# State space of both layers: products moved from GpSimd to VectorE, responses a step behind their matrices, state copies on ScalarE, first layer's output due inside the first branch

## The chip, the core and the metric

The kernel runs on one core of a Trainium2 chip. Its metric is the device time of one execution in microseconds. The engines are called by the profile's names: PE is TensorE (matmuls; PEld its weight loads), DVE is VectorE, ACT is ScalarE, POOL is GpSimd, SP is SyncE, which here issues nearly all DMAs. An engine runs its instructions in the order in which they were written for it; semaphores join the engines.

## The reference

One inference step of a two-layer model on 128 context tokens and 512 latent tokens, all in fp32, 1024 channels. Per layer: an adaLN modulation, one wide projection, three mixers beside each other (retention, a bidirectional state space model, attention), three branch projections joined by sigmoid gates, an output projection with a LayerNorm, and a gated FFN with a convolution over three tokens and another LayerNorm.

```
z = (x * (1 + sc1) + sh1) @ w_in           # rq rk rv rg | su | nq nk nv | gates
r_out = retention(rq, rk, rv, rg, ...)
s_out = s5(su, ...)
n_out = attention(nq, nk, nv, ...)
m = (ga*(r_out@w_branch[0]) + gb*(s_out@w_branch[1]) + gc*(n_out@w_branch[2])) @ w_o
x = layer_norm(ALPHA*x + g1*m)
f = conv_ffn(x * (1 + sc2) + sh2)
x = layer_norm(ALPHA*x + g2*f)
```

The change is about `s5`: 32 groups of 16 channels, 64 complex states per group and direction. Per group and direction the state follows h(t) = a_bar h(t-1) + b_bar u(t) and the output is Re(C h(t)) + D u(t); then a GELU and a gate `y * sigmoid(y @ w_glu)` (GLU).

## The kernel before

**Main work.** fp32 weights come from HBM as 128x1024 tiles (`raw`), are split into a high part (ACT, L176) and a low part (DVE, L177), and PE multiplies three combinations of parts (L148). A unit of this work is 48 matmuls of 128x320 into one of two PSUM buffers `pa`, then an evacuation on ACT or DVE. `layer` writes down the list of units of a layer: projections for retention and the state space, gates of branch 0, branch 0, GLU, gates and branch 1, attention's projections, branch 2, output projection, FFN.

**Side work.** Retention, attention and the state space are generators. They are carried forward beside the units: each unit has a cost (1 for a usual one), and a generator with rate r makes r steps per unit cost. `RATE_S` is the rate of layer 0's state space, `RATE_P` that of layer 1's preparation (`ssm_prep(1)`), which runs during layer 0's FFN. An action with `need=[ssm]` runs the generator to its end first. A list scheduler then fixes the order of instructions on each engine when the kernel is built; it simulates durations and keeps dependences.

**The state space.** The 640 tokens are cut into 80 chunks of 8. `ssm_powers` computes powers of a_bar. `ssm_entry` (8 batches of 4 groups) makes the matrices that bring a chunk's inputs into the state: six operations of 128x512 (`cmul`, L899 to L904, tiles `eo` and `etm`), then two DMAs to DRAM (`ed`, L1076). In layer 0 these run on DVE except batch 3 (`ENTRY_POOL`), in layer 1 on POOL. `ssm_exit` prepares `bb` by six operations on POOL, then for each batch makes the matrices from states to outputs by six operations of 128x640 on POOL (L1105 to L1110, `go` and `gtm`), stores them (`gd`), and right behind them has PE compute the responses within a chunk from these (16 matmuls, L1119), which DVE collects into `tb` (L1125 to L1129) and SP stores. `ssm_states` multiplies each batch by `ed` on PE (L1161) and copies the results into the state tile H: real parts on DVE (L1167 to L1170), imaginary parts on ACT (L1166). The scan then takes 64 steps of four operations on DVE (L1184 to L1187). `ssm_outputs`: in four groups of eight, H is copied into `hs` (DVE for the real part, ACT for the imaginary one, L1214 to L1218), `gm` is loaded, PE multiplies (L1228, L1230), DVE evacuates into `ym` (L1231), and SP stores eight `yd` (L1235). `ssm_out` loads `yt`, takes the GELU on ACT and splits it (`gyhi`, `gylo`); GLU's matmuls (L1263) read that. In layer 0, `first_ssm` runs the powers, then entry and states beside exit, then the outputs. `ssm_out` is written down behind gate 5 of branch 0.

**Other places of POOL.** Retention's rotation multiplies by the cosine on POOL (L606) and scales queries by decays there (`qd`, L625). In the merge, branch 0's result is written to a tile `mg` by DVE (L1308), branch 1's is added to it on POOL (L1310), branch 2's on DVE (L1312).

In layer 0's FFN the adaLN of layer 1 also runs: weights `in_w_adaT` are loaded as `raw` tiles by SP and multiplied by a row on DVE (L308). The FFN's own evacuation is the convolution (`cv`, L1381) on DVE.

## Time and profile before

| | |
|---|---|
| three runs | 2592.34, 2592.64, 2585.28 us (median 2592.34) |
| profiled execution | 2584.16 us, its span 2582.3, so 1.9 outside the span |
| mean granted clock | 0.974 |
| busy in the span | PE 2416.7 (94%), DVE 1809.3 (70%), ACT 954.7 (37%), POOL 482.5 (19%) |
| instructions | PE 17788, DVE 4043, ACT 1649, POOL 336 |

The stages by time: 0 to 65 us the start; 65 to 402 layer 0's projections, retention and state space; 402 to 968 branches, attention, output projection; 968 to 1240 layer 0's FFN up to its end part; then layer 1, whose states and outputs run beside its projections. A clock of 1.0 in the profile is 2.4 GHz.

### The profile page before, as it was taken

The numbers are of one execution on the slowest core, as the hardware profiler recorded it, in microseconds if no ns is written. First come the engines' busy times: TensorE is split into PE (matmuls) and PEld (weight loads), VectorE is DVE, ScalarE is ACT, GpSimd is POOL, SyncE is SP. The second block draws the span as 40 slices with busy tenths as digits, with TensorE's granted clock in tenths as the row PEclk, the third lists the DMA queues.
The fourth block names the chain that finished last, engine by engine and source line by source line (L and its number), as shares of the span: only waits on it lengthen the run. The fifth ranks groups of instructions, "written<-read, shape, count | busy, mean of one in ns | idle before, by whom it ended". The sixth has DMA issues, their size and how long they took to land. (4 is left out here: it accounts for less than half of the span.)

```text
span 2582.3 us, 45009 instructions
## 1 busy us (share of the span) xinstructions
PE 2416.7 (94%) x17788; PEld 2342.7 (91%) x17788; DVE 1809.3 (70%) x4043; ACT 954.7 (37%) x1649; POOL 482.5 (19%) x336
## 2 busy tenths in 40 slices
PE   7879999899999997989999999989989989999997
PEld 4769999899899997979999999989988989999997
DVE  5997965785367896798665578478545788555657
ACT  3245333136543432313234543421656243232232
POOL 1555101221200007492000210102213200000001
PEclk9889999999999999999999999999999999999999
DMA  8653535552223337345335323555222343222222
GB/s 286 174 173 112 171 95 162 182 162 80 77 91 123 113 108 220 123 131 151 119 99 186 99 92 103 159 176 168 93 87 79 111 127 115 86 62 86 84 76 79
DMA packets 174083, 324.04 MB, mean 125 GB/s; under 512 B 35120, under 2 KB 84528, under 8 KB 173872
## 3 DMA queue, kind: packets, MB, share of 16 engines
q1 hardware_dynamic: 173440, 321.03, 39.5%
q8 instruction: 140, 2.29, 0.4%
q14 instruction: 71, 0.58, 0.1%
q10 hardware_dynamic: 432, 0.13, 0.0%
HBM read 287.09 MB, written 38.21 MB: 126 GB/s over the span
## 5 line engine op out<-in xcount | busy, mean ns | idle before, releaser
L148 PE MATMUL pa<-hth,hi 128*128 128x320 f32 (+2 forms) x2896 | 689.7, 316 | 49.3 <-DVE cv L1381 21.9
L148 PE MATMUL pa<-htl,hi 128*128 128x320 f32 (+2 forms) x2896 | 686.4, 315 | 1.2 <-DVE htl L461 0.8
L148 PE MATMUL pa<-hth,lo 128*128 128x320 f32 (+2 forms) x2896 | 686.0, 314 | 1.5 <-DVE lo L177 1.5
L176 ACT ACTIVATE hi<-raw 128x1024 fp32r<-128x1024 f32 (+1 forms) x316 | 322.2, 1022 | 840.9 <-PE pa L148 336.8
L177 DVE TENSOR_TENSOR lo<-raw,hi 128x1024 fp32r<-128x1024 f32 (+1 forms) x316 | 406.1, 1287 | 289.5 <-ACT hi L176 282.2
L148 PEld LDWEIGHTS pa<-hth,hi 128*128 128x128 f32 x2896 | 496.6, 192 | 59.1 <-issue 26.3
L148 PEld LDWEIGHTS pa<-htl,hi 128*128 128x128 f32 x2896 | 496.3, 191 | 9.1 <-issue 3.0
L148 PEld LDWEIGHTS pa<-hth,lo 128*128 128x128 f32 x2896 | 497.6, 192 | 7.4 <-issue 5.4
L308 DVE SCALAR_TENSOR_TENSOR junk<-raw,crow 128x512 bf16<-128x512 f32 x320 | 249.8, 781 | 53.1 <-DMA raw<-in_w_adaT 48.5
L1338 PE MATMUL b<-lo,hdh 128*128 128x256 f32 x784 | 218.8, 281 | 1.2 <-DVE lo L177 1.1
L1337 PE MATMUL b<-hi,hdh 128*128 128x256 f32 x784 | 216.7, 282 | 3.0 <-DVE rm L1341 1.9
L1339 PE MATMUL b<-hi,hdl 128*128 128x256 f32 x784 | 217.7, 281 | 0.0
L1381 DVE SCALAR_TENSOR_TENSOR cv<-pa,conv,cv 128x641 f32<-128x641 f32 (+3 forms) x180 | 153.1, 852 | 3.6 <-ACT cv L1377 1.5
L1337 PEld LDWEIGHTS b<-hi,hdh 128*128 128x128 f32 x784 | 146.1, 188 | 5.3 <-DVE rm L1341 1.8
L1338 PEld LDWEIGHTS b<-lo,hdh 128*128 128x128 f32 x784 | 147.7, 188 | 1.9 <-DVE lo L177 1.7
L1339 PEld LDWEIGHTS b<-hi,hdl 128*128 128x128 f32 x784 | 147.1, 188 | 0.2 <-issue 0.2
L1341 DVE TENSOR_TENSOR rm<-b,g 128x256 f32<-128x256 f32 x168 | 69.0, 418 | 71.9 <-PE b L1339 69.8
L431 POOL TENSOR_TENSOR x<-x,ln_b 128x512 f32<-128x512 f32 x4 | 6.5, 1660 | 521.2 <-ACT x L430 521.2
L516 PE MATMUL pa<-lo,hth 128*128 128x256 f32 x320 | 91.8, 288 | 2.7 <-DVE lo L177 2.7
L515 PE MATMUL pa<-hi,hth 128*128 128x256 f32 x320 | 93.2, 294 | 1.0 <-ACT rw L1488 1.0
L517 PE MATMUL pa<-hi,htl 128*128 128x256 f32 x320 | 91.2, 288 | 0.0
L176 ACT ACTIVATE hdh<-cv 128x641 fp32r<-128x641 f32 x44 | 32.6, 742 | 143.0 <-DVE cv L1389 132.4
(404 smaller groups left out, 4403.9 us busy)
## 6 DMA issues: line engine op xcount, KB each, us to landing
raw<-in_w_in_a SPq DMA_DIRECT2D x96, 512.0 KB
raw<-in_w_up SPq DMA_DIRECT2D x88, 512.0 KB
raw<-in_w_adaT SPq DMA_DIRECT2D x80, 512.0 KB
raw<-in_w_down SPq DMA_DIRECT2D x36, 512.0 KB
raw<-in_w_branch SPq DMA_DIRECT2D x24, 512.0 KB
raw<-in_w_o SPq DMA_DIRECT2D x24, 512.0 KB
wada<-in_w_ada SPq DMA_DIRECT2D x32, 256.0 KB
raw<-in_w_in_b SPq DMA_DIRECT2D x16, 512.0 KB
```

Of the source, the lines that this page charges most:

```text
L148: s.nc.tensor.matmul(ps[h][:, :n], w[a][:, k], x[b][:, k, c0:c0 + n], start=(k == 0 and part == 0), stop=(k == nk - 1 and part == 2))
L176: s.nc.scalar.activation(hi, src, AF.Copy)
L177: return (eng or s.nc.vector).tensor_tensor(lo, src, hi.bitcast(FT), op=OP.subtract)
L308: nc.vector.scalar_tensor_tensor(junk, w[:, n], 1.0, s.crow[j], op0=OP.mult, op1=OP.mult, accum_out=acc[:, n, j:j + 1])
L515: mm(ps, h[0], x[0], start=(k == 0), stop=False)
L516: mm(ps, h[0], x[1], start=False, stop=False)
L517: mm(ps, h[1], x[0], start=False, stop=(k == 7))
L1337: mm(ps, a[0], x[0], start=(k == 0), stop=False)
L1338: mm(ps, a[0], x[1], start=False, stop=False)
L1339: mm(ps, a[1], x[0], start=False, stop=(k == nk - 1))
L1341: nc.vector.tensor_tensor(m, ps, g[0 if t == 0 else 1][:, 256 * (q % 2):256 * (q % 2) + 256], op=OP.mult)
L1381: nc.vector.scalar_tensor_tensor(x[:, o0:o1], z[:, z0:z0 + o1 - o0], cw(tap), x[:, o0:o1], op0=OP.mult, op1=OP.add)
```

## The change

- Moved from POOL to DVE: the matrices of the exit (`go`, `gtm`, 48 operations per layer), the `bb` preparation (6 per layer), all entry products that were on POOL (6 in layer 0, 48 in layer 1), the product with the cosine (8 per layer) and `qd` (8 per layer), and branch 1's addition (8 per layer).
- `ssm_exit`: matrices of batch b and responses of batch b - 1 make one step; nine steps instead of eight, and `go` of two batches are alive at a time.
- All copies into H and `hs` go to ACT, in both layers.
- Layer 0's `ssm_out` is written down behind the second unit of branch 0, not behind gate 5 (layer 1's stays).
- Branch 0's result stays in its gate tile; the tile for the sum (`ms`) is allocated at branch 1.
- `RATE_S` 1.5 to 1.4 and `RATE_P` 0.6 to 0.5.

```diff
--- before.py
+++ after.py
@@ -605,3 +605,3 @@
             V.tensor_tensor(t1, t1, s.sin, op=OP.mult)
-            G.tensor_tensor(x[:, LP:T], x[:, LP:T], s.cos, op=OP.mult)
+            V.tensor_tensor(x[:, LP:T], x[:, LP:T], s.cos, op=OP.mult)
             V.tensor_tensor(x[:, LP:T], x[:, LP:T], t1, op=OP.add)
@@ -624,3 +624,3 @@
         for d in range(2):
-            G.tensor_tensor(qd[d], q[:, LP:T].rearrange("p (t n) -> p t n", t=4),
+            V.tensor_tensor(qd[d], q[:, LP:T].rearrange("p (t n) -> p t n", t=4),
                             m[:, 2 + d:3 + d].to_broadcast([P, 4, 128]), op=OP.mult)
@@ -1055,3 +1055,2 @@
         nc, V, G, A = s.nc, s.nc.vector, s.nc.gpsimd, s.A
-        on = lambda b: G if l or b in ENTRY_POOL else V
         pd, ed = s.ssm[l]["pd"], s.ssm[l]["ed"]
@@ -1073,3 +1072,3 @@
             tm = s.unit([P, 4, 2, 64], base="etm")
-            s.cmul(on(b), o, pm, [x[:, :, None, :].to_broadcast([P, 4, 2, 64]) for x in be], tm)
+            s.cmul(V, o, pm, [x[:, :, None, :].to_broadcast([P, 4, 2, 64]) for x in be], tm)
             for i in range(2):
@@ -1094,8 +1093,8 @@
             G.memset(bb[i][:, GR], 0.0)
-        s.cmul(G, [x[:, :GR] for x in bb], bs, [f[:, i, :, None].to_broadcast([P, GR, 16]) for i in range(2)], tm)
+        s.cmul(V, [x[:, :GR] for x in bb], bs, [f[:, i, :, None].to_broadcast([P, GR, 16]) for i in range(2)], tm)
         s.free(bs, tm)
         yield
-        for b in range(8):
-            g0 = 4 * b
+        def matrices(b):
 
+            g0 = 4 * b
             o = [s.unit([P, 4, 10, 16], base="go") for _ in range(2)]
@@ -1104,8 +1103,8 @@
             cv = [x[:, g0:g0 + 4, None, :].to_broadcast([P, 4, 10, 16]) for x in ct]
-            G.tensor_tensor(o[0], cv[0], pv[0], op=OP.mult)
-            G.tensor_tensor(tm, cv[1], pv[1], op=OP.mult)
-            G.tensor_tensor(o[0], o[0], tm, op=OP.add)
-            G.tensor_tensor(o[1], cv[0], pv[1], op=OP.mult)
-            G.tensor_tensor(tm, cv[1], pv[0], op=OP.mult)
-            G.tensor_tensor(o[1], o[1], tm, op=OP.subtract)
+            V.tensor_tensor(o[0], cv[0], pv[0], op=OP.mult)
+            V.tensor_tensor(tm, cv[1], pv[1], op=OP.mult)
+            V.tensor_tensor(o[0], o[0], tm, op=OP.add)
+            V.tensor_tensor(o[1], cv[0], pv[1], op=OP.mult)
+            V.tensor_tensor(tm, cv[1], pv[0], op=OP.mult)
+            V.tensor_tensor(o[1], o[1], tm, op=OP.subtract)
             for i in range(2):
@@ -1113,3 +1112,8 @@
                                     o[i][:, :, 1:9].rearrange("p g k c -> p g (k c)"))
+            s.free(tm)
+            return o
 
+        def responses(b, o):
+
+            g0 = 4 * b
             ps = [s.bank([P, 128]) for _ in range(2)]
@@ -1130,3 +1134,10 @@
             nc.sync.dma_start(td[g0:g0 + 4].rearrange("g c t -> (g c) t"), tb)
-            s.free(o, tm, tb)
+            s.free(o, tb)
+        o = None
+        for b in range(9):
+
+            new = matrices(b) if b < 8 else None
+            if b:
+                responses(b - 1, o)
+            o = new
             yield
@@ -1162,6 +1173,4 @@
             for i in range(2):
-                E = V.tensor_copy
+                E = lambda o, x: nc.scalar.activation(o, x, AF.Copy)
                 hv = H[:, i].rearrange("p n g -> p g n")[:, 4 * b:4 * b + 4]
-                if i:
-                    E = lambda o, x: nc.scalar.activation(o, x, AF.Copy)
                 E(hv[:64, :, 1:17], ps[i][:64, :, 0:16])
@@ -1213,3 +1222,3 @@
                 hv = H[:, i].rearrange("p n g -> p g n")[:, 8 * gb:8 * gb + 8]
-                E = (lambda o, x: nc.scalar.activation(o, x, AF.Copy)) if i else V.tensor_copy
+                E = lambda o, x: nc.scalar.activation(o, x, AF.Copy)
                 E(hs[i][:64, :, 0:16], hv[:64, :, 0:16])
@@ -1291,4 +1300,3 @@
             if b == 0 and i == 0:
-                s.mT = []
-                s.mg = s.cp.tile([P, 8, T], FT, name=s.name("mg"), tag="x")
+                s.mT, s.mg = [], {}
             out = (s.rout, s.sout, s.nout)[b]
@@ -1305,9 +1313,14 @@
                 t = s.gts.pop((b, ct))
-                m = s.mg[:, ct]
-                o = t if b else m
-                nc.vector.scalar_tensor_tensor(s.both(o), s.both(t), 1.0, s.two(ps), op0=OP.add, op1=OP.mult)
+                nc.vector.scalar_tensor_tensor(s.both(t), s.both(t), 1.0, s.two(ps), op0=OP.add, op1=OP.mult)
+                if b == 0:
+                    s.mg[ct] = t
+                    continue
                 if b == 1:
-                    nc.gpsimd.tensor_tensor(m, m, t, op=OP.add)
+                    if ct == 0:
+                        s.ms = s.cp.tile([P, 8, T], FT, name=s.name("mg"), tag="x")
+                    m = s.mg.pop(ct)
+                    nc.vector.tensor_tensor(s.ms[:, ct], m, t, op=OP.add)
+                    s.free(m)
                 if b == 2:
-                    nc.vector.tensor_tensor(t, t, m, op=OP.add)
+                    nc.vector.tensor_tensor(t, t, s.ms[:, ct], op=OP.add)
                     s.dump(f"mT{ct}", t)
@@ -1555,3 +1568,3 @@
             add(s.gate_unit(l, 0, c))
-            if c == 5:
+            if c == 5 and l:
                 add(s.action(s.ssm_out, need=[ssm]))
@@ -1559,2 +1572,4 @@
             add(s.branch_unit(l, 0, i))
+            if i == 1 and not l:
+                add(s.action(s.ssm_out, need=[ssm]))
         for i in range(2):
@@ -1752,3 +1767,3 @@
 
-TAIL, ENTRY_POOL = (0, 1), (3,)
+TAIL = (0, 1)
 
@@ -1758,3 +1773,3 @@
 
-RATE_R, RATE_N, RATE_S, RATE_T, RATE_P = 2.5, 2.75, 1.5, 0.7, 0.6
+RATE_R, RATE_N, RATE_S, RATE_T, RATE_P = 2.5, 2.75, 1.4, 0.7, 0.5
 
```

In the kernel after, line numbers are up to 15 higher: exit's products are L1104 to L1109, the responses' collection L1129 to L1133, the scan L1193 to L1196, output matmuls L1237 and L1239, branches L1310.

DVE where layer 0's scan begins, before. `tb` is the last batch of responses, `H` the state tile, `lo` weight splits:

```order
L1127 TENSOR_TENSOR tb_2678<-tb_2678,b_2660 128x16
L1129 SCALAR_TENSOR_TENSOR tb_2678<-cst,sp_dc_588,tb_2678 128x16
L177 TENSOR_TENSOR lo_2644<-raw_2364,hi_2643 128x1024
L1167 COPY H_1503<-b_2688 64x4x16
L1168 COPY H_1503<-b_2688 64x4x64
L1169 COPY H_1503<-b_2688 64x4x16
L1170 COPY H_1503<-b_2688 64x4x64
L177 TENSOR_TENSOR lo_2976<-raw_2498,hi_2975 128x1024
L1186 TENSOR_TENSOR H_1503<-H_1503,rc_452_2706 128x2x2x32
L1187 TENSOR_TENSOR H_1503<-H_1503,rc_453_2707 128x2x2x32
```

and after, the same place:

```order
L677 BN_AGGR rmv_2678<-rbst_2677 128x2 x4
L1131 TENSOR_TENSOR tb_2885<-tb_2885,b_2867 128x16
L1108 TENSOR_TENSOR gtm_3036<-ct_810,px_634 128x640
L184 TENSOR_SCALAR rsw_2691<-rmv_2678 128x5
L1133 SCALAR_TENSOR_TENSOR tb_2885<-cst,sp_dc_641,tb_2885 128x16
L1109 TENSOR_TENSOR go_3035<-go_3035,gtm_3036 128x640
L185 TENSOR_SCALAR rrs_2679<-rsw_2691 128x5
L188 TENSOR_TENSOR rst_2690<-rrs_2679 128x5
L189 SCALAR_TENSOR_TENSOR rst_2690<-rst_2690,rsw_2691 128x5
L190 SCALAR_TENSOR_TENSOR rst_2690<-rst_2690 128x5
L191 SCALAR_TENSOR_TENSOR rrs_2679<-rst_2690,rrs_2679 128x5
L1195 TENSOR_TENSOR H_1710<-H_1710,rc_478_2913 128x2x2x32
```

Before, the last batch's copies into H and no matrices precede the scan on DVE; after, the last batch's matrices (`go`, `gtm`) and its responses stand there, retention's norm (`rsw`, `rrs`, `rst`) between them, and no copy.

SP in layer 0's FFN, before. `eo` to `ed` are stores of entry matrices, `epm` and `ebe` their operands, `raw` weights:

```order
L1076 DMA ed_10367<-eo_10937 128x512
L1076 DMA ed_10367<-eo_10789 128x512
L1065 DMA epm_11240<-pd_10219 128x1x512
L206 DMA raw_10959<-in_w_adaT 128x1024
L1065 DMA epm_11239<-pd_10218 128x1x512
L1069 DMA ebe_11390<-in_b_entry_re 128x1x256
L1069 DMA ebe_11390<-in_b_entry_im 128x1x256
L1076 DMA ed_10367<-eo_10938 128x512
```

and after, the same place:

```order
L1075 DMA ed_10488<-eo_11072 128x512
L206 DMA raw_11083<-in_w_up 128x1024
L1075 DMA ed_10488<-eo_11073 128x512
L206 DMA raw_11201<-in_w_adaT 128x1024
L1068 DMA ebe_11205<-in_b_entry_re 128x1x256
L1068 DMA ebe_11205<-in_b_entry_im 128x1x256
L1064 DMA epm_11505<-pd_10340 128x1x512
L206 DMA raw_11230<-in_w_up 128x1024
```

Two stores of `eo` in a row stand ahead of a load of `in_w_adaT` before; after, each store has a load of `in_w_up` behind it, and the load of `in_w_adaT` comes behind both.

PE in layer 0's outputs, between two of the four groups (`ut` inputs, `hs` states, `gm` matrices), before:

```order
L1230 MATMUL b_3902<-hs_3866,gm_3897 128x80
L1228 MATMUL b_3902<-ut_1508,gm_3898 128x80
L1230 MATMUL b_3902<-hs_3865,gm_3896 128x80
L1230 MATMUL b_3902<-hs_3866,gm_3897 128x80
L148 MATMUL pa_4245<-hth_165,hi_4150 128x320 x2
L148 MATMUL pa_4245<-htl_166,hi_4150 128x320 x2
L148 MATMUL pa_4245<-hth_165,lo_4151 128x320 x2
L148 MATMUL pa_4245<-hth_165,hi_4150 128x320 x2
L148 MATMUL pa_4245<-htl_166,hi_4150 128x320 x2
```

and after, between two groups:

```order
L1237 MATMUL b_4016<-ut_1715,gm_4012 128x80
L1239 MATMUL b_4016<-hs_3979,gm_4010 128x80
L1239 MATMUL b_4016<-hs_3980,gm_4011 128x80
L1237 MATMUL b_4016<-ut_1715,gm_4012 128x80
L1239 MATMUL b_4016<-hs_3979,gm_4010 128x80
L1239 MATMUL b_4016<-hs_3980,gm_4011 128x80
L1237 MATMUL b_4112<-ut_1717,gm_4108 128x80
L1239 MATMUL b_4112<-hs_4095,gm_4106 128x80
L1239 MATMUL b_4112<-hs_4096,gm_4107 128x80
```

Before, a gate's unit (`pa`) follows the group; after, the next group follows at once, as it does until branch 0.

## Rows read from the trace of the kernel before

**Rows 1.** Windows: busy us (instructions) by engine, clock, DMA share, GB/s.

```profile
65.00:270.00 205.00, 169.19 (x1345) 160.01 (x1344) 176.20 (x409) 78.27 (x152) 109.81 (x66) 0.89 0.51 153
...
65.00:402.00 337.00, 297.77 (x2308) 287.22 (x2307) 272.76 (x750) 124.81 (x215) 121.43 (x75) 0.93 0.49 149
968.00:1240.00 272.00, 241.78 (x1924) 235.10 (x1923) 216.57 (x330) 65.67 (x77) 157.65 (x101) 0.96 0.51 157
1240.00:1700.00 460.00, 454.42 (x3385) 452.21 (x3385) 302.01 (x792) 189.41 (x300) 33.25 (x23) 1.00 0.39 124
```

**Rows 2.** The page's slices: POOL, busy tenths in 40 equal slices.

```profile
POOL 1555101221200007492000210102213200000001
```

**Rows 3.** PE's waits, 65 to 402 us: releaser, total us, times, longest.

```profile
PE b L1119 <- POOL go L1107: 8.2, 2, 7.7
PE b L1119 <- POOL go L1110: 7.7, 3, 6.8
```

**Rows 4.** PE's waits, 968 to 1240 us.

```profile
PE pa L148 <- DVE cv L1381: 21.0, 4, 11.6
PE b L1119 <- POOL go L1110: 4.0, 2, 3.1
```

**Rows 5.** Timeline of DVE, two places: start us, us, instruction.

```profile
90.09 0.68 DVE L899 TENSOR_TENSOR eo<-epm,ebe 128x512 f32<-128x512 f32 x1
90.69 0.68 DVE L902 TENSOR_TENSOR eo<-epm,ebe 128x512 f32<-128x512 f32 x1
...
95.78 1.32 DVE L891 TENSOR_TENSOR sp_q<-sp_q,ex_t 128x32 f32<-128x32 f32 x1
...
130.40 0.18 DVE L891 TENSOR_TENSOR sp_q<-sp_q,ex_t 128x32 f32<-128x32 f32 x1
```

**Rows 6.** Timeline of POOL, 88 to 100 us.

```profile
93.73 3.32 POOL L899 TENSOR_TENSOR eo<-epm,ebe 128x512 f32<-128x512 f32 x1 [3.62 <-DMA epm<-pd]
```

**Rows 7.** DVE's forms, 65 to 270 us: busy us, mean ns, idle before.

```profile
L891 DVE TENSOR_TENSOR sp_q<-sp_q,ex_t 128x32 f32<-128x32 f32 x8 | 7.6, 954 | 0.0
...
L1129 DVE SCALAR_TENSOR_TENSOR tb<-cst,sp_dc,tb 128x16 f32<-128x16 f32 x7 | 5.3, 764 | 0.1
...
L1170 DVE COPY H<-b 64x256 f32<-64x256 f32 x8 | 4.9, 608 | 0.0
...
L892 DVE TENSOR_SCALAR sp_q<-sp_q 128x32 f32<-128x32 f32 x8 | 4.8, 594 | 0.0
```

**Rows 8.** DVE's forms, 968 to 1240 us.

```profile
L308 DVE SCALAR_TENSOR_TENSOR junk<-raw,crow 128x512 bf16<-128x512 f32 x48 | 48.0, 999 | 27.3 <-DMA raw<-in_w_adaT 26.8
```

**Rows 9.** DVE's forms, whole span.

```profile
L705 DVE TENSOR_TENSOR ro<-ro,rgt 128x640 f32<-128x640 f32 x8 | 6.5, 817 | 0.0
```

**Rows 10.** The scan's last operation L1187: ns min/median/max, first and last start.

```profile
L1187 DVE TENSOR_TENSOR H<-H,rc x64: 214/225/1311, 271.5 to 367.6; 128x64 f32<-128x64 f32 x48, 128x128 f32<-128x128 f32 x16
```

**Rows 11.** ACT's lines, 65 to 402 us.

```profile
L1214 ACT ACTIVATE hs<-H 64x128 f32<-64x128 f32 (+1 forms) x16 | 12.5, 790 | 12.2 <-DVE H L1187 6.0 <-DMA out_new_state_ssm<-fo 3.2 <-DMA yd<-ym 2.9
```

**Rows 12.** Timeline of PE in the outputs.

```profile
387.17 0.61 PE L1230 MATMUL b<-hs,gm 128*128 128x80 f32 x4
...
387.84 0.61 PE L1230 MATMUL b<-hs,gm 128*128 128x80 f32 x4
```

**Rows 13.** Timeline of SP's queue in the outputs.

```profile
372.95 10.15 SPq L1235 DMA_DIRECT2D yd<-ym  x16
```

**Rows 14.** Branch 0's matmuls L1302: ns min/median/max, first and last start.

```profile
L1302 PE MATMUL pa<-rohi,hi x64: 307/309/421, 402.1 to 429.7; 128*128 128x320 f32 x64
```

**Rows 15.** Output matmuls L1230, then the last split of the GELU on DVE.

```profile
L1230 PE MATMUL b<-hs,gm x128: 230/275/275, 365.8 to 397.6; 128*128 128x80 f32 x128
...
409.60 1.14 DVE L177 TENSOR_TENSOR gylo<-gy,gyhi 128x640 fp32r<-128x640 f32 x1 [0.46 <-ACT gyhi L176]
```

**Rows 16.** SP's waits, 968 to 1030 us.

```profile
SPq L1076 <- POOL eo L901: 14.1, 6, 5.9
```

**Rows 17.** DVE's waits, 968 to 1240 us.

```profile
DVE junk L308 <- DMA raw<-in_w_adaT: 26.8, 9, 11.1
```

## The prediction

> **What bounds the kernel now.** The windows come first [rows 1], because the share of the whole span hides the stages. From 1240 to 1700 us PE is busy 454.4 of 460 us at full clock: nothing to win there. Two stretches are different: 65 to 402 us (layer 0's state space, beside projections and retention) and 968 to 1240 us (layer 0's FFN, beside layer 1's state space preparation). In both DVE is the fullest engine after PE or ahead of it: 176.2 of 205 us against PE's 169.2 between 65 and 270, and 216.6 of 272 later. PE runs there at clock 0.89 and 0.96. The page's POOL line [rows 2] is thick in these two places and almost empty elsewhere. The waits of PE [rows 3] name POOL's matrices (`go`) for 8.2 us in two waits and 7.7 in three in the first stretch; in the second they name a DVE evacuation (`cv`, 21.0 us in 4 waits) and POOL for 4.0 [rows 4].
>
> **Why DVE is so full.** The same DVE instruction has two durations. An `eo` multiply takes 0.68 us and the next starts 0.60 after it; `L891`, on 32 columns, takes 0.18 us at 130.40 and 1.32 at 95.78 [rows 5], where a POOL instruction of 3.32 us is under way [rows 6]. By form the means lie far above the undisturbed value: `L891` 954 ns against 180, `L892` 594, `L1129` 764 [rows 7]. I priced every form of 65 to 270 (111 groups, 409 instructions) at the value it has where POOL is still: 59 us too much (the three named make 6.2 + 3.4 + 3.8; `L892`'s and `L1129`'s undisturbed values are taken as 0.17 and 0.22). The same between 968 and 1240 gives 62 us; `L308` at 999 ns (0.69 undisturbed) is 15 of it [rows 8]. I take it that DVE waits for POOL there; when POOL's two-operand work leaves, these waits leave.
>
> **The front, 65 to 402 us.** DVE gets 48 matrix operations (8 batches of 6) and 28 others ahead of the scan (6 `eo`, 6 `bb`, 8 for the cosine, 8 `qd`). An operation of 128x512 costs 0.60 (start to start, above), so 28 make 16.8. For 128x640 no such product stands on DVE before; a product of that size from two SBUF operands takes 817 ns [rows 9], 0.75 from start to start if 640/512 of 0.60: 48 make 36.0. The 32 copies into H that go to ScalarE take 14 us off (the largest, `L1170`, 608 ns [rows 7]). Sum +39. DVE's load to 270 becomes 176.2 - 59 + 39 = 156, and with the 28.8 us in which it idled there the scan starts at 65 + 156 + 29 = 250, not at 271.5 [rows 10]. The 64 steps last 97 us before; ScalarE takes the `hs` copies off DVE (5 us) and 7 us of the stretch from 270 to 372 are such waits, but some 4 us of other DVE work falls behind: 89. ScalarE does the copies more slowly, as its rows show (790 ns a copy of `hs` [rows 11]); I count 3 us, since only the first group delays PE. Then come 32 output groups. In PE's new order no projection stands between them, and a group takes 0.67 us (387.17 is one, 387.84 the next [rows 12]): 21.4. SP issues a `yd` store every 0.65 us (10.15 for 16 [rows 13]), and loads of `gm` stand behind 8 of them: 5 more. So branch 0 starts at 250 + 89 + 3 + 27 = 369, against 402.1 [rows 14]; two of the 33 us I leave for new short waits of PE on DVE, and one for rounding. **Front: -30.** Bounds: with PE's 39 idle us (337 less 297.8 [rows 1]) and 15 of the 24 that the clock cost ((1 - 0.93) x 337) gone -54; with half of DVE's 59 us still there about zero; with all of it there +27, the scan starting at 309.
>
> The late due time of the first layer's output: before, the GELU and the split of it must be issued ahead of the last gates; now they may come while branch 0 runs, 28 us of PE work [rows 14], and the chain from the last output matmul (397.6) to the end of the last split (410.7) lasts 13 [rows 15]. It is covered; if not, GLU waits up to 10. The rate of 1.4 instead of 1.5 lets the steps be asked for 7% later; I count it as nothing, since DVE's load and not the asking sets the scan's start here. Steps of matrices and responses apart cost PE nothing by themselves: PE's responses have a whole step to wait for DVE. They hold two more `go` tiles for longer, which I cost at nothing because units are also freed earlier by the shorter chain.
>
> **The FFN of layer 0.** DVE gets 54 operations at 0.60 (48 `eo`, 6 `bb`) and 48 at 0.75: 68. It loses 62 of waits: 216.6 - 62 + 68 = 223 of 272, the same load. But none of the operations is stretched any more when an evacuation stands behind them, `SP`'s stores of `eo` no longer wait for POOL (14.1 us in 6 waits [rows 16]), behind which the weight loads of `in_w_adaT` stand, for which in turn DVE waits (26.8 in 9 [rows 17]); the 11-us wait of PE on `cv` is the end of that chain. At a rate of 0.5 instead of 0.6 the 27 steps cover 54 units of PE's cost instead of 45, of 62. Of 25.0 us of named waits and 11 us of clock ((1 - 0.96) x 272) I take 25 + 7, less 6 for new waits on a DVE that is as full as before. **FFN: -26.** Bounds: -36 (all) and +13 (the waits on the port stay: 216.6 + 68 = 285, over 272).
>
> The Trainium skill, "Perfetto Trace Analysis", section "Optimizing Scalar/DVE Operations", says to move work off VectorE, even to GpSimd, when VectorE is saturated, and warns that the two share an SBUF port so that such a move may not help. By its first half this change goes the wrong way, and the front would come out at +27; its warning fits rows 5 to 7, where a 32-column operation takes seven times as long beside POOL, and by that half the work costs VectorE less when it does it itself.
>
> **Elsewhere: 0.** The merge's additions (16 of 128x640 moved from POOL, half of them per layer) come where PE waits for weights; DVE is busy 302 of 460 from 1240 on [rows 1] and gets 8 x 0.75 = 6 us. Keeping branch 0 in its gate tiles costs no instruction. Layer 1's copies to ScalarE fall on an engine that is busy 189 of 460 there. Should the added ScalarE work delay weight splits, I bound it by 16 copies of 0.79, 13 us, at most half on the path.
>
> **Sum.** 2584.2 - 30 - 26 = 2528 by the profiled execution. The median of the runs shown lies 8 us above it (2592.3), the lowest 1 above; I add half: **2532**. On its own this case ranges from 2505 to 2556. What can be told from no change is 0.3%, about 8 us.
>
> **The rivals.**
> - *DVE becomes the bound* (slower). If the long durations are not POOL's doing, the added 39 and 68 us land on an engine already full: the scan starts at 309, branch 0 at 429, +27, and the FFN +13: 2628. It decides where fewer than about 29 of the 59 us vanish. For it: DVE at 176 of 205. Against: the short and the long duration of one form [rows 5], and POOL's line [rows 2]. Chance 0.08.
> - *The output chain takes the gain back.* Outputs now run with nothing beside them; if the loads of `gm` wait for all 32 `yd` stores (21 us rather than 5) and GLU for its input 10 us, the front gives 4 instead of 30: 2558. For it: SP's 10.15 us in one piece. Against: a store of one group needs no load of the next to wait long. Chance 0.14.
> - *The FFN's waits only change their name.* PE waits for `cv` behind `L308`, whose weights stand on SP behind a store of `eo`; the store now waits for DVE instead of POOL. The front alone: 2558. Chance 0.10.
> - *Both of these*, 2584 to 2588, no change: 0.04.
> - *All losses go.* PE is the only bound in both stretches: 2584 - 54 - 36 + 4, about 2500. Chance 0.08.
> - The forecast, 0.56.
>
> Faster by over 0.3%: 0.56 + 0.14 + 0.10 + 0.08, less 0.02 for the edges: 0.86. The same: 0.05. Slower: 0.09. The range goes from the last rival to beyond the second and third, 2498 to 2578; what is left out above is the first rival and the case of no change.
>
> **What the profile after would show.** DVE's `L891`, `L892` and the H steps near 0.2 us throughout; POOL almost empty from 65 to 270 and 968 to 1240; the scan starting near 250 and branch 0 near 370; PE's clock over 0.93 before 270; no `cv` wait of 11 us in the FFN; DVE still near 220 of 270 us there. Wrong would be: matrix operations on DVE at well over 0.82 us, a scan that starts after 271, outputs with waits for `gm` or `hs` above 10 us, or PE waits for `cv` of 20 us as before.

## The result

| | before | after |
|---|---|---|
| median of runs | 2589.76 us (4 runs, 2585.28 to 2592.64) | 2561.09 us (4 runs, 2558.63 to 2565.84) |
| profiled span | 2582.3 us | 2559.0 us |
| mean granted clock | 0.974 | 0.971 |

The ratio is 0.9893 with a 95% interval of 0.9871 to 0.9915: 1.1% faster, a little under half of the 2.3% that was forecast, at a time inside the stated range (2498 to 2578 us). The spans differ by 23.3 us. By stages, from the first matmul of each stage in the two timelines (the last down projections, which share the buffer `pa` with layer 1's first units, are counted to the rest):

| stage | before | after | gained |
|---|---|---|---|
| up to GLU of layer 0 | 430.4 | 430.9 | -0.5 |
| GLU to the first down projection of layer 0's FFN | 494.5 | 487.4 | 7.1 |
| down projections of layer 0, first to last (layer 1 is prepared beside them) | 418.0 | 400.2 | 17.8 |
| the rest (layer 1) | 1239.4 | 1240.5 | -1.1 |

So the FFN gave two thirds of what was forecast, the front nothing, and the merge something that was not forecast.

**What the change did to VectorE** shows as predicted. POOL's line on the page answers to [rows 2]:

```profile
POOL 1000000011200000000000000010113200000001
```

VectorE's forms between 65 and 270 us, to be read against [rows 7] and [rows 9] (count, busy us and mean ns behind the bar):

```profile
L1109 DVE TENSOR_TENSOR go<-go,gtm 128x640 f32<-128x640 f32 x8 | 6.6, 821 | 0.0
...
L891 DVE TENSOR_TENSOR sp_q<-sp_q,ex_t 128x32 f32<-128x32 f32 x8 | 1.5, 188 | 0.0
...
L1133 DVE SCALAR_TENSOR_TENSOR tb<-cst,sp_dc,tb 128x16 f32<-128x16 f32 x6 | 1.4, 234 | 0.1
...
L892 DVE TENSOR_SCALAR sp_q<-sp_q 128x32 f32<-128x32 f32 x8 | 1.4, 180 | 0.0
```

`L891` falls from 954 to 188 ns, `L892` from 594 to 180, `L1129` (now `L1133`) from 764 to 234, and a matrix operation takes 821 ns, as the row of its size promised. With POOL still, VectorE takes on the 39 us of work that the prediction counts for this stretch and is busy less than before. The Trainium skill, "SBUF — State Buffer", section "Who interferes with whom", says that a VectorE instruction with two SBUF inputs contends with a GpSimd instruction that reads SBUF, over a shared port pair that it calls an exclusive lock; `L891` has two such inputs and agrees (954 to 188 ns).

That POOL's work stretched them, and none of the other edits, shows in two runs that come below. e3 moves the products and changes nothing else; e4 is the changed kernel with the products back on POOL. `L891` between 65 and 270 us, in e3 and then in e4:

```profile
L891 DVE TENSOR_TENSOR sp_q<-sp_q,ex_t 128x32 f32<-128x32 f32 x8 | 1.4, 180 | 0.0
```
```profile
L891 DVE TENSOR_TENSOR sp_q<-sp_q,ex_t 128x32 f32<-128x32 f32 x8 | 4.8, 596 | 0.0
```

The windows, answering to [rows 1] (the columns are the same; the second row is the stretch of the outputs, and the row by itself below is that stretch before):

```profile
65.00:270.00 205.00, 184.28 (x1526) 177.81 (x1527) 160.85 (x471) 96.31 (x199) 0.00 (x0) 0.93 0.56 167
...
372.00:402.00 30.00, 30.00 (x140) 30.00 (x139) 4.72 (x9) 13.68 (x16) 1.54 (x1) 0.50 0.50 145
...
968.00:1240.00 272.00, 256.78 (x2028) 251.70 (x2027) 236.60 (x455) 72.87 (x85) 0.22 (x2) 0.99 0.52 155
```
```profile
372.00:402.00 30.00, 28.70 (x226) 28.32 (x225) 8.41 (x16) 11.28 (x13) 2.45 (x2) 1.00 0.59 185
```

VectorE's 160.9 us up to 270 are near the 156 forecast, and PE does 15 us more in that time. But from 372 to 402 PE is busy all the time at a granted clock of 0.50, the lower level (1.2 GHz); before it was 1.00 there.

**Where the front's gain went.** PE had it. Before, PE came to the outputs at 365.8 us [rows 15] with two gates, 14.1 us of work, still to do; after, it has done these at 353.1: a lead of 26.8 us. The timeline of PE from there (start, duration, instruction; in brackets how long PE was idle before it, and whom it waited for):

```profile
352.65 0.45 PE L148 MATMUL pa<-hth,lo 128*128 128x320 f32 x2
358.06 1.14 PE L1239 MATMUL b<-hs,gm 128*128 128x80 f32 x4 [4.96 <-ACT hs L1223]
360.23 0.72 PE L1239 MATMUL b<-hs,gm 128*128 128x80 f32 x2 [1.03 <-ACT hs L1223]
360.74 0.63 PE L1237 MATMUL b<-ut,gm 128*128 128x80 f32 x2
...
362.02 0.63 PE L1237 MATMUL b<-ut,gm 128*128 128x80 f32 x2
...
398.65 0.88 PE L1310 MATMUL pa<-rohi,hi 128*128 128x320 f32 x2
...
403.06 0.47 PE L1310 MATMUL pa<-rohi,lo 128*128 128x320 f32 x2
```

PE pauses 4.96 and 1.03 us for the `hs` copies on ScalarE. From then on a group of three output matmuls (each has two records) takes 1.28 us (360.74 to 362.02) where it took 0.67 [rows 12], and the first of branch 0's take 0.73 a pair until 403, then 0.46. From the last gate to branch 0 it is 45.5 us, not 21.4. The windows show that the clock falls inside the pause: PE does nothing in the two middle rows, and the first matmul behind the pause comes at 358.06, after the fall.

```profile
340.00:350.00 10.00, 10.00 (x70) 10.00 (x69) 8.27 (x36) 1.50 (x2) 0.00 (x0) 1.00 0.23 72
...
353.20:355.20 2.00, 0.00 (x0) 0.00 (x0) 1.26 (x2) 0.70 (x1) 0.00 (x0) 1.00 0.00 0
355.40:358.00 2.60, 0.00 (x0) 0.00 (x0) 1.11 (x7) 2.13 (x2) 0.00 (x0) 0.50 0.64 195
...
360.00:370.00 10.00, 9.77 (x46) 9.77 (x47) 0.98 (x2) 9.86 (x13) 0.00 (x0) 0.50 0.14 30
```

Against the 21.4, that is 6.0 us of pauses and 18.1 of half clock too much; of a lead of 26.8, 3.4 is left when branch 0 begins at 398.65 ([rows 14]: 402.1). Its own start at half clock and a wait of 1.7 us for a gate take that too.

The scan's end, for [rows 10]:

```profile
L1196 DVE TENSOR_TENSOR H<-H,rc x64: 218/225/294, 268.3 to 356.4; 128x64 f32<-128x64 f32 x48, 128x128 f32<-128x128 f32 x16
```

It begins at 268.3, not at 250, and lasts 88 us, where 89 were forecast. PE was through with its gates 3.5 us before it ended (356.6).

**FFN.** For [rows 4], [rows 17] and [rows 8], PE's wait, VectorE's wait and VectorE's form in 968 to 1240:

```profile
PE pa L148 <- DVE cv L1394: 10.4, 6, 4.8
```
```profile
DVE junk L308 <- DMA raw<-in_w_adaT: 13.3, 9, 5.0
```
```profile
L308 DVE SCALAR_TENSOR_TENSOR junk<-raw,crow 128x512 bf16<-128x512 f32 x56 | 38.5, 688 | 13.7 <-DMA raw<-in_w_adaT 13.3
```

PE's wait on `cv` halves (21.0 to 10.4), the one on matrices (4.0) is gone, VectorE's for `in_w_adaT` halves (26.8 to 13.3), and `L308` takes 688 ns, not 999. VectorE is busy 236.6 of these 272 us, where 223 were forecast. Layer 0's down projections alone take 418.0 us before, so the 272 us that the prediction read are only a part of that stage.

### The profile page after: what moved, and what is told of

It is laid out like the page before. It is cut to its first block, busy times and chain, and to the rows that moved or that the text cites. A ratio compares the mean times of both kernels' runs of the same rounds, so it can differ in the third digit from the quotient of the medians.

```text
span 2559.0 us, 44900 instructions
## 1 busy us (share of the span) xinstructions
PE 2426.2 (95%) x17788; PEld 2352.5 (92%) x17788; DVE 1759.2 (69%) x4157; ACT 1000.4 (39%) x1745; POOL 137.9 (5%) x126
## 5 line engine op out<-in xcount | busy, mean ns | idle before, releaser
L177 DVE TENSOR_TENSOR lo<-raw,hi 128x1024 fp32r<-128x1024 f32 (+1 forms) x316 | 376.3, 1192 | 289.8 <-ACT hi L176 282.3
L308 DVE SCALAR_TENSOR_TENSOR junk<-raw,crow 128x512 bf16<-128x512 f32 x320 | 226.5, 708 | 29.2 <-DMA raw<-in_w_adaT 25.4
L1390 ACT ACTIVATE cv<-pa,conv 128x641 f32<-128x641 f32 (+2 forms) x90 | 76.5, 850 | 18.1 <-PE pa L148 18.1
```

Of the source, the lines that this page charges most:

```text
L177: return (eng or s.nc.vector).tensor_tensor(lo, src, hi.bitcast(FT), op=OP.subtract)
L308: nc.vector.scalar_tensor_tensor(junk, w[:, n], 1.0, s.crow[j], op0=OP.mult, op1=OP.mult, accum_out=acc[:, n, j:j + 1])
L1390: nc.scalar.activation(x[:, a:b], z[:, a - base:b - base], AF.Identity, scale=cw(1), bias=cw(3))
```

## Experiments: why the outputs ran at half clock

Theory A: a pause of PE lowers its clock, and the small output matmuls behind it go on at the lower level. Theory B: 96 matmuls of 80 columns in a row lower it whatever stands before them. Theory C: the front's lead is lost later in any case.

**e1, the pause filled.** Gate 7's product is computed twice (7.0 us more), branch 0 is held behind the last output, and `ssm_out` is written down ahead of branch 0.

```diff
-            s.project([ps[:, h] for h in range(2)], w, 8, s.hT, s.SP2)
+            for _ in range(times):     # 2 for gate 7 of branch 0, layer 0
+                s.project([ps[:, h] for h in range(2)], w, 8, s.hT, s.SP2)
...
+            if gb == 3 and not l:
+                s.after = s.small([P, 1], 'after', 1)
+                V.tensor_copy(s.after, ym[:, 7, :1])
...
+                if (l, b, i) == (0, 0, 0):
+                    nc.vector.tensor_copy(ps[:, 0, :1], s.after)
...
+        if not l:
+            add(s.action(s.ssm_out, need=[ssm]))
         for i in range(4):
             add(s.branch_unit(l, 0, i))
-            if i == 1 and not l:
-                add(s.action(s.ssm_out, need=[ssm]))
```

> The changed kernel with gate 7 of layer 0's branch 0 multiplied twice (same result, 7.0 us more PE work ahead of the outputs) and branch 0's first PSUM tile touched by DVE after the last output, so that the 32 output groups still stand in one piece. Theory A (PE pauses 6.0 us for ScalarE's hs copies, the granted clock falls to 0.50 behind that pause, and the outputs take 40.5 us in place of 21.4): the pause is filled, the clock stays 1.00, outputs take 21 to 23 us, total 2561 - 6 - 19 - 4 + 7 = 2539 us. Theory B (96 matmuls of 80 columns in a row lower the clock, whatever stands before them): clock 0.50 and 40 us again, only the pause goes, 2561 - 6 + 7 = 2562 us. Theory C (the lead of the front is lost at GLU or in the merge in any case): outputs at full clock but 2561 + 7 = 2568 us.

Measured: 2566.34 us, ratio to before 0.9915 (0.9898 to 0.9932). The time lies between B's 2562 and C's 2568, but the profile is none of the three: the pause only moved. PE's timeline and windows of e1:

```profile
369.75 0.61 PE L1240 MATMUL b<-hs,gm 128*128 128x80 f32 x4
...
370.43 0.61 PE L1240 MATMUL b<-hs,gm 128*128 128x80 f32 x4
...
371.50 0.40 PE L148 MATMUL pa<-hth,lo 128*128 128x320 f32 x1
381.46 0.69 PE L1238 MATMUL b<-ut,gm 128*128 128x80 f32 x2 [9.56 <-DMA gm<-md]
...
382.79 0.64 PE L1238 MATMUL b<-ut,gm 128*128 128x80 f32 x2
...
384.07 0.64 PE L1238 MATMUL b<-ut,gm 128*128 128x80 f32 x2
```
```profile
360.00:370.00 10.00, 10.00 (x89) 10.00 (x87) 1.47 (x3) 9.87 (x12) 0.00 (x0) 1.00 0.11 26
...
380.00:390.00 10.00, 8.54 (x40) 8.57 (x41) 0.49 (x1) 0.00 (x0) 0.00 (x0) 0.50 0.94 331
```

The first half of the outputs runs without a pause for 10 us: 0.67 us a group, clock 1.00. Then PE waits 9.56 us for `gm`, whose loads stand on SP behind 16 `yd` stores (11.0 us), and behind that a group takes 1.28. Here too the clock falls inside the pause: it is 1.00 from 371.50 to 373.30 and 0.50 from 373.50 to 381.40, with no matmul in the second of these windows.

**e5, also that pause taken away.** As e1, with layer 0's `yd` stores issued by GpSimd:

```diff
-                nc.sync.dma_start(s.yd[8 * gb + j].rearrange("c l n -> l c n"), ym[:, j])
+                (nc.sync if l else nc.gpsimd).dma_start(s.yd[8 * gb + j].rearrange("c l n -> l c n"), ym[:, j])
```

> As e1_no_pause, but layer 0's 32 yd stores are issued by GpSimd, so that the loads of gm no longer stand behind 16 of them on SP (in e1 that made PE pause 9.6 us between the second and the third group, and the clock, at 1.00 through the first 10 us of outputs, was 0.50 behind it). Theory A (a pause lowers the clock, and the 80-column matmuls behind it run at it): no pause, 1.00 throughout, the outputs take 21 to 23 us in one piece; total 2566 - 9 - 14 - 4 = 2537 to 2545 us. Theory B (96 matmuls of 80 columns in a row lower it without a pause): the first 10 us at 1.00, then 0.50; total 2550 to 2560.

Measured: 2559.88 us, ratio 0.9888 (0.9868 to 0.9908); as a time it is the upper end of B's 2550 to 2560. The windows from 368 on and the two pauses that were left:

```profile
368.00:372.00 4.00, 4.00 (x38) 4.00 (x37) 1.84 (x3) 3.95 (x6) 3.05 (x6) 1.00 1.03 350
372.00:376.00 4.00, 1.33 (x11) 1.05 (x9) 0.53 (x2) 3.95 (x7) 3.43 (x6) 1.00 0.99 288
376.00:380.00 4.00, 3.52 (x16) 3.38 (x16) 0.00 (x0) 1.05 (x2) 1.26 (x3) 0.50 1.00 364
```
```profile
374.27 0.42 PE L1238 MATMUL b<-ut,gm 128*128 128x80 f32 x2 [1.36 <-DMA gm<-md]
376.49 1.35 PE L1240 MATMUL b<-hs,gm 128*128 128x80 f32 x4 [1.79 <-ACT hs L1224]
```

The outputs ran for 13 us at 1.00 (a few of gate 7's 320-column matmuls stand among the first), then paused twice, 1.36 for `gm` and 1.79 for `hs`, and only behind these went on at 0.50. Outputs in one piece for all of their 21 us without any pause were not reached, so B is not excluded for the last 8 us; in e1 and e5 it did not happen before a pause, and in the changed kernel the clock had fallen before the first output.

**e2, the outputs elsewhere.** Two empty steps ahead of the outputs; what comes earlier is unchanged.

```diff
         yield from s.beside(itertools.chain(s.ssm_entry(0), s.ssm_states(0)), s.ssm_exit(0))
+        for _ in range(2):
+            yield
         yield from s.ssm_outputs(0)
```

> The changed kernel with two more empty steps ahead of layer 0's outputs: everything up to there stays in place, the outputs move 5 to 25 us of PE work later, in pieces between branch 0's matmuls. Theory A: no pause, clock 1.00 through the outputs, branch 0's end 24 to 29 us earlier; total 2532 us, up to 2541 if GLU then waits for its input. Theory B: pieces of 80-column matmuls stand between 320-column ones, clock 1.00 as well: also 2532 to 2541. Theory C: no gain, 2556 to 2566.

Measured: 2539.42 us, ratio 0.9811 (0.9794 to 0.9827), 22 us below the changed kernel by one edit. The windows of the outputs in e2:

```profile
350.00:360.00 10.00, 9.78 (x67) 9.51 (x65) 8.15 (x35) 2.18 (x3) 0.00 (x0) 1.00 0.24 65
360.00:370.00 10.00, 9.31 (x76) 9.31 (x77) 1.98 (x5) 9.85 (x11) 0.00 (x0) 1.00 0.23 76
...
380.00:390.00 10.00, 10.00 (x82) 10.00 (x80) 2.54 (x3) 2.86 (x4) 0.00 (x0) 1.00 0.97 359
```

PE goes from the gates into branch 0, takes the outputs in two pieces from 362 on, and the clock stays at 1.00; GLU begins at 406.2, 24.7 us earlier than in the changed kernel. A and B had the same forecast for this run, so it does not tell them apart; C falls, though not entirely. From GLU to the first down projection e2 takes 491.7 us and the changed kernel 487.4, so 4.3 of the 24.7 are spent again there. In e5 GLU begins 6.1 us earlier (424.8), that stretch takes 494.3, and the lead is gone. What limits PE there was not tried.

**e11, no step apart.** Matrices and responses of one batch in one step again. This also moves the outputs: by the order they stand in two pieces, with 72 of branch 0's matmuls between.

```diff
-        o = None
-        for b in range(9):
-            new = matrices(b) if b < 8 else None
-            if b:
-                responses(b - 1, o)
-            o = new
-            yield
+        for b in range(8):
+            responses(b, matrices(b))
+            yield
```

> The changed kernel with matrices and responses of a batch in one step again. The outputs fall between branch 0's matmuls by this order, so the front's half clock should be gone as in e2. If the step apart is worth nothing else: 2539 to 2545. If it saves PE waits for go (predicted at nothing): waits of 10 us or more on go come on top, in the front and in layer 0's FFN, 2550 to 2565.

Measured: 2553.72 us, ratio 0.986 (0.9845 to 0.9874). The time lies in the second range, but for a reason that was not expected: pieces are not safe by themselves. This is the run that tells a pause from many small matmuls in a row. PE's waits from 65 to 430 and its windows:

```profile
PE b L1234 <- ACT hs L1218: 4.4, 2, 2.9
...
PE b L1123 <- DVE go L1109: 5.3, 1, 5.3
PE b L637 <- DVE tb L1129: 4.8, 1, 4.8
```
```profile
360.00:370.00 10.00, 6.80 (x33) 6.65 (x33) 1.31 (x2) 9.84 (x12) 0.00 (x0) 0.62 0.17 54
370.00:380.00 10.00, 10.00 (x49) 10.00 (x48) 0.98 (x2) 7.46 (x12) 0.00 (x0) 0.50 0.16 40
...
390.00:400.00 10.00, 10.00 (x82) 10.00 (x82) 3.36 (x4) 1.06 (x1) 0.00 (x0) 1.00 0.87 300
```

The first piece follows 2.94 and 1.51 us of waits for `hs` and runs at 0.50 to its end; branch 0's 320-column matmuls bring the clock back, and the second piece of the same size, entered without a pause, runs at 1.00. As to the step apart itself: waits of 5.3 for `go` and 4.8 for `tb` take the place of the changed kernel's one of 11.7, so it is worth little in the front; the down projections take 399.0 us (changed kernel 400.2). In the changed kernel its main effect is where it puts the outputs.

**e3, the moves alone, and e4, the rest alone.**

```diff
 e3 (against the kernel before)
-            G.tensor_tensor(o[0], cv[0], pv[0], op=OP.mult)
+            V.tensor_tensor(o[0], cv[0], pv[0], op=OP.mult)
...
-        on = lambda b: G if l or b in ENTRY_POOL else V
+        on = lambda b: V
...
-                    nc.gpsimd.tensor_tensor(m, m, t, op=OP.add)
+                    nc.vector.tensor_tensor(m, m, t, op=OP.add)
 e4 (against the kernel after): the same lines the other way
```

> The kernel before with only the products moved from GpSimd to VectorE (exit's matrices and preparation, entries, cosine, qd, branch 1's addition); no step apart, copies shared as before, output due at gate 5, rates 1.5 and 0.6. The outputs stand in one piece here too, 14 us of PE work earlier. Theory A: VectorE's waits beside GpSimd go (the long forms fall to their short values), the lead at 320 us is 25 us or more, and is lost again behind a pause ahead of the outputs with the clock at 0.50; FFN gains 15: total 2565 to 2575. If the moves alone carry everything: 2561. If the gain came from the other edits: 2590.

> The changed kernel with the products back on GpSimd: step apart, copies on ScalarE, later due time, gate tiles and rates stay. Theory that the moves carry the gain: VectorE's long forms are back, FFN's cv waits too, 2585 to 2600. Rival, that the order and the copies carry it: 2561 to 2570.

Measured: e3 2560.95 us, ratio 0.9891 (0.9871 to 0.9911); e4 2614.46, 1.0095 (1.0072 to 1.0117). The moves carry all of the change's gain, and the other edits by themselves cost 27 us; with the moves they come to nothing on balance. By theory A I had e3 at 2565 to 2575; the time is the one expected if the moves carry everything (2561). Its front is lost behind a pause of 5.9 us and half clock as expected, but layer 1 was faster than I knew (1230.8 us for the rest behind the down projections, 1239.4 before; e3's profiled execution took 2553.66 us). e4 was worse than expected; its stretch of down projections takes 431 us against 418 before, and what in it does that was not tried.

**e12, the rates back** to 1.5 and 0.6 in the changed kernel.

> The changed kernel with the rates of the kernel before (1.5 and 0.6). The outputs then stand 14 us of PE work earlier, in one piece, ahead of the last two gates. By theory A: a pause of about the same length, as the states come earlier too, clock 0.50 through the outputs, total within 5 us of the changed kernel, 2556 to 2566. If the rates carry part of the gain (FFN: fewer products a unit): 2566 to 2580.

Measured: 2578.45 us, ratio 0.9957 (0.9941 to 0.9973): 17 us slower than the changed kernel, in the range of the second expectation, but mostly in the front and not in the FFN: GLU begins at 445.0, 14.1 us later. PE's waits of e12:

```profile
PE pa L515 <- ACT qk L1481: 14.4, 2, 10.0
PE b L1239 <- ACT hs L1223: 9.2, 2, 8.1
```

The pause ahead of the outputs is longer (8.12 and 1.03), the clock behind it 0.50 again, and retention's projections now wait 14.4 us for evacuations on ScalarE. The down projections take 404.9 in place of 400.2. The two rates together, of which the prediction counted the first at nothing, are worth 17 us beside these moves.

## Experiments: the stages that I counted at nothing

**e6, copies shared again** between VectorE and ScalarE, in both layers:

```diff
-                E = lambda o, x: nc.scalar.activation(o, x, AF.Copy)
+                E = V.tensor_copy if i == 0 else lambda o, x: nc.scalar.activation(o, x, AF.Copy)
```

> The changed kernel with the real parts of H and hs copied by VectorE again in both layers. If ScalarE's copies alone make the pause ahead of layer 0's outputs: the pause falls from 6.0 us to about 2, the clock stays, 2535 to 2545. If the scan's end makes most of it (PE was through with its work at 353.1, the scan ended at 356.7): a pause of 4 to 5 us stays, clock 0.50 as in the changed kernel, 2556 to 2562.

Measured: 2545.31 us, ratio 0.9837 (0.9817 to 0.9857), 16 us below the changed kernel, though the pause stays (4.32 us) and so does the half clock: the profile is that of the second expectation, and the gain comes from elsewhere. In the profiles the last state matmul of layer 0 ends 5.5 us earlier (260.1 against 265.6), and layer 1 from its first state matmul to branch 2 takes 585.1 us in place of 596.9. ScalarE's copies there, in the changed kernel and in e6:

```profile
L1174 ACT ACTIVATE H<-b 64x64 f32<-64x64 f32 x64 | 24.2, 459 | 2.0 <-PE b L1172 1.2 <-DMA ut<-ud 0.5
L1223 ACT ACTIVATE hs<-H 64x128 f32<-64x128 f32 (+1 forms) x32 | 24.0, 772 | 3.0 <-DVE H L1196 1.1 <-DVE rolo L708 0.9 <-DMA nvd<-nvt 0.7
```
```profile
L1223 ACT ACTIVATE hs<-H 64x128 f32<-64x128 f32 (+1 forms) x16 | 12.2, 786 | 4.9 <-PE b L1239 2.5 <-DVE H L1196 1.4 <-DVE rolo L708 0.9
L1174 ACT ACTIVATE H<-b 64x64 f32<-64x64 f32 (+1 forms) x32 | 12.1, 461 | 1.8 <-PE b L1172 1.7
```

In the changed kernel 24 us more of ScalarE work stand between its evacuations and weight splits, for nothing: VectorE had room. In e3, e9 and e10, which share the copies, that stretch takes 584 to 588 us, in the eight others with the products on VectorE 592 to 597. Which of ScalarE's instructions came late there, the runs do not single out.

**e7, the merge tile as before, and e8, branch 1's addition on GpSimd:**

```diff
 e7
-                s.mT, s.mg = [], {}
+                s.mT = []
+                s.ms = s.cp.tile([P, 8, T], FT, name=s.name("mg"), tag="x")
...
+                o = s.ms[:, ct] if b == 0 else t
...
-                    nc.vector.tensor_tensor(s.ms[:, ct], m, t, op=OP.add)
+                    nc.vector.tensor_tensor(s.ms[:, ct], s.ms[:, ct], t, op=OP.add)
 e8
-                    nc.vector.tensor_tensor(s.ms[:, ct], m, t, op=OP.add)
+                    nc.gpsimd.tensor_tensor(s.ms[:, ct], m, t, op=OP.add)
```

> The changed kernel with branch 0's result written to the merge tile again in both layers (gate tiles come free at once; branch 1's addition stays on VectorE). In the run of the moves alone, layer 1 from its states to branch 2 took 588 us against 597 in the changed kernel. Theory that the gate tiles held longer delay the merge: 2551 to 2556. Rival (the difference is not there): 2561.

> The changed kernel with branch 1's addition back on GpSimd. From GLU to attention the changed kernel is 7 us ahead of the kernel before, where I had counted nothing. If the addition on VectorE does it: 2568. If it is something else (weights that come earlier): 2561.

Measured: e7 2561.85 us (ratio 0.9902, 0.9883 to 0.9922), no difference from the changed kernel; e8 2570.48 (0.9928, 0.9911 to 0.9944), 9 us slower. Holding gate tiles costs nothing, as I had it; the addition on VectorE is worth 9 us, which I had at nothing. From GLU to layer 0's first down projection e8 takes 493.4 us, the changed kernel 487.4; the rest of the 9 lies mostly behind the down projections, where layer 1 has the same additions (1242.8 against 1240.5).

## A faster version

**e9** has e2's two steps and e6's copies.

> Both gains together: the outputs two steps later (e2) and the real parts' copies back on VectorE in both layers (e6). If they are independent: e2's 2539 less the 11 us that e6 gained in layer 1, and 4 of the 5 in layer 0's states: 2524 to 2530. If e6's gain needs the outputs in one piece: 2536 to 2541.

Measured: 2530.25 us, ratio to before 0.9772 (0.9755 to 0.9789), the fastest kernel here, 31 us below the changed one and at the upper end of the first range, as if the two gains were independent. No half clock in the outputs:

```profile
100.00:160.00 60.00, 40.13 (x310) 37.65 (x309) 51.99 (x134) 21.80 (x40) 0.00 (x0) 0.77 0.66 201
...
360.00:370.00 10.00, 10.00 (x89) 10.00 (x88) 5.70 (x13) 6.49 (x9) 0.00 (x0) 1.00 0.42 113
...
380.00:390.00 10.00, 10.00 (x92) 10.00 (x91) 1.48 (x3) 1.35 (x2) 0.00 (x0) 1.00 0.86 301
```

The row of 100 to 160 is the largest loss left in the front: PE is idle for 19.9 us, 12.8 of them in one wait for the first matrices, with the clock at 0.77.

**e10** tries that, with layer 0's exit beginning later (against e9):

```diff
-            if n % 2:
+            if n % 2 and n > 2:
                 next(b, None)
...
-        for _ in range(2):
+        for _ in range(4):
```

> As e9, with layer 0's exit beginning two steps of entry later (and the outputs held back two more steps, so that they stay between branch 0's matmuls). All kernels with the products on VectorE have one PE pause of 11 to 13 us near 113 us, for the matrices of the first batch (go), with the clock at 0.77 from 100 to 160. If this pause is only that VectorE has too much queued at that time: it shrinks to 5 or less and the total is 8 to 15 us below e9. Rival: the pause moves to another batch or to the cosine (qk), and the total is e9's within 4 us.

Measured: 2536.17 us, ratio 0.9793 (0.9772 to 0.9813), 5.9 us slower than e9. The wait for `go` is gone, but retention's projections wait 11.6 us for an evacuation on ScalarE (`qk`) instead: the pause moved, as the rival had it, though the total is outside its 4 us. A second loss was not expected. The outputs run for 7.5 us at 1.00, wait 1.86 us for `gm`, and go on at 0.50 until branch 0's matmuls come:

```profile
364.00:371.80 7.80, 7.80 (x70) 7.74 (x68) 3.75 (x8) 4.36 (x6) 0.00 (x0) 1.00 0.42 142
...
373.80:378.80 5.00, 5.00 (x24) 5.00 (x24) 0.24 (x1) 1.13 (x2) 0.00 (x0) 0.50 0.23 55
```

## Why the prediction was wrong

- *What bounds the kernel*: right. The two stretches, VectorE's waits beside POOL, and that they go with POOL's work; VectorE's load came out at 161 us (156 forecast) and PE's lead at 27 (30).
- *The front's outputs*: wrong, and this is the step that failed. "32 output groups ... a group takes 0.67 us ...: 21.4" was read from a stretch at full clock, which PE entered from 320-column matmuls with a wait of only 0.73 us (the line below). I added 3 us for the copies and 5 for loads as waits, but not what a wait does to the clock behind it. From the scan's end to branch 0 I had 30 us (3 + 27), and it was 42; from the last gate it was 45.5 (6.0 of pauses, 39.5 of outputs). The excerpt of PE's order had shown that the next group follows at once; this was priced as a chain, at an unchanged rate.

```profile
386.92 0.42 PE L1228 MATMUL b<-ut,gm 128*128 128x80 f32 x2 [0.73 <-DMA gm<-md]
```

- *The scan's start*: wrong, 268.3 for 250. I kept the 28.8 us in which VectorE idled before; up to 268.3 it idled 44 (203.3 less 159.2 busy). "DVE's load and not the asking sets the scan's start" was not so: the last state matmul ends at 265.6, and VectorE stands idle 2.1 us for the last copy into H, on ScalarE, right ahead of the scan. The same operation of the scan comes at 265.6 with the old rates (e12), at 263.6 with the copies shared (e6) and at 257.8 with the moves alone (e3); so the rate and the copies have a part in it, and the rest is not singled out. By itself this cost PE little: the gates stand ahead of the outputs in PE's order and were done at 353.1, so by an estimate (353.1 and 21.4) branch 0 could not have begun before 374.5 at any start of the scan. But it put the scan's end 3.5 us behind the last gate, and so made the pause.
- *FFN*: right in kind, mis-sized: -17.8 for -26. 10.4 us of `cv` waits stayed, where I took 25 of 25 and gave 6 back; VectorE was fuller than I had it (236.6 us for 223).
- *Elsewhere 0*: several errors that partly cancel. The merge's addition on VectorE is worth 9 us (e8), and the moves gain in layer 1, where I had nothing (e3, 8.6 us in its profile); the copies on ScalarE cost 16 (e6), some 11 of them behind the down projections, where I had bounded them by half of 13. By stages the two places gained 6.0 us together (7.1 less 1.1). The rate's zero was wrong too: 17 us with the FFN's rate (e12).
- *Rivals and signs*: the time came out as "the output chain takes the gain back" (2558), but by another mechanism: no output waited for `gm` in the changed kernel's layer 0 nor GLU for its input. No rival has the clock fall in the outputs, so it is luck that the range holds the time. None of the signs of being wrong appeared either (821 ns a matrix operation, a scan before 271, 6.0 us of waits for `hs`, 10.4 for `cv`): they look for waits, and the loss was in the matmuls behind a short one.

The runs bear out theory A in this form: the clock fell in a pause, or within 1 us behind it (e4, e8, e11), and the small matmuls behind it ran on at 0.50. The Trainium skill, "TensorE: Matmul & The Clock Gate", section "Part 1: The HAM clock gate", says that the throttled state is the default and activity releases it. The runs agree in part: the clock is 0.50 behind pauses of 1.86 us (e10), 0.68 and 1.51 (e4), 2.94 and 1.51 (e11), 4.96 and 1.03 (the changed kernel), and 1.00 again once 320-column matmuls run; but 38 us of unbroken 80-column matmuls in the changed kernel did not release it. Nor does every pause lower it: the waits of 0.57 and 0.73 us in the outputs of before passed at 1.00, and so did one of 2.86 us for `cv` between 320-column matmuls in the changed kernel's FFN (until 1049.65).

## What to carry to other kernels

When a change brings work nearer to the end of a serial chain, price the matmuls behind the chain at both clocks: here pauses of 6.0 us ahead of small matmuls cost three times their own length on top (18.1). Read whether PE will enter such a stretch from large matmuls or from a wait, and if from a wait, put it a few units later, where large matmuls surround it. A rate or an order that the profile of before shows as harmless is priced for the engines' load of before, so after a move of load it has to be set anew.

## What was not expected of the hardware

- Branch 0's 320-column matmuls, entered at half clock, ran so for 4.4 us (398.65 to 403.06) and then at full clock; the 80-column ones stayed at 0.50 for 38 us with PE busy all that time.
- The same piece of 80-column matmuls entered from large ones without a pause ran at 1.00 for 10 us (e1) and 13 us (e5). A wait of 1.86 us in the middle of such a piece was enough for 0.50 behind it (e10).
- Operations on 32 columns with one SBUF operand and a constant (`L892`) were stretched beside POOL as those with two were: 594 to 180 ns, and 595 with the products back on POOL (e4).
